# Moving the modulation and gate products beside the gate projections, and reordering the even attention

## The chip, the cores and the metric

One Trainium2 chip, one core. The time is device microseconds of one execution of the whole program, the median of several. Engines: TensorE (PE, matmuls; PEld are its weight loads), VectorE (DVE), ScalarE (ACT), GpSimd (POOL), and SyncE (SP), whose queue issues most of the loads.

## What is computed

Two layers of a diffusion backbone, on 128 prompt tokens and 512 latent tokens, width 1024. The change is in the first (even) layer and in products that the layers' modulation needs. Cut to that:

```python
def layer(x, cvec, l, ctx):
    shift, scale, gate = split(silu(cvec) @ ada_w + ada_b, 3)      # per layer: 1024 -> 3 x 1024
    h = rmsnorm(x, norm_g) * (1.0 + scale) + shift
    out = even_mix(h, ...) or odd_mix(h, ...)
    return x + gate * out

def even_mix(h, ...):
    cq, ckv, kr, g_a, q_b, k_b, v_b, g_b = split_cols(h @ w_in)
    # 8 heads of latent attention (keys of 64 + 32 columns), 8 grouped-query heads (64 columns, 2 key heads)
    o_a = attend(q_a, k_a, v_a) * silu(g_a)        # latent tokens read 128 cached + 512 own keys,
    o_b = attend(q_b, k_b, v_b) * silu(g_b)        # prompt tokens read the 128 prompt keys only
    return concat(o_a, o_b) @ w_out
```

## The kernel before

The program runs stage after stage: modulation of the even layer and its input projections (to 148 us), the gate projections (`even_gates`, L589), the even attention (`attention`, L697), the output projection with the odd layer's norm (`out_proj`, `mid`, from 374 us), then the odd layer. Matrix products in fp32 are made of three products of rounded high and low parts (`mm3`, `lin_feat`): each weight tile of 128 x 1024 is loaded into `raw` (three buffers, taken in turn by all that loads into it), rounded into `whi` on ScalarE (L76), and the rest goes into `wlo` on VectorE, or on GpSimd where `lo_on` says so (L77); then its `raw` buffer is free.

`even_gates` makes eight chunks of 48 matmuls (`lin_feat`, L120), a tanh and a multiply into `og`. Nothing else runs on TensorE there but a few query transposes.

The modulation products of the odd layer are in `ada_cols` (L179): two loads of 512 KB into two `raw` buffers, eight fp32 matmuls on 32-column tiles (L186; 16 records), a copy (L189), and, as the function `rest`, two transposes (L193) and a reduction (L195). The gate vector's product is `ada_gate_part` (L221; one 512 KB load, eight matmuls of 128 columns, L230, a copy), eight times, and `ada_gate_row` sums it and sends it to memory. All of these are issued in the attention: `side(h)` (L863) is called after the value run of head h and issues one `ada_cols` for h below 7 (one more ahead of the first head), and from head 8 on the gate products, the splits `op_split` of the first half of the output's operand (a cast on ScalarE, L890, a subtraction on GpSimd, L891), and from head 12 on one load of output weights each with its low part on GpSimd.

The attention goes over 16 heads (8 latent, 8 grouped). For a head, a score tile (`head_scores`: six matmuls of 320 columns, L619, in latent heads, four in grouped ones) covers 128 of the 512 queries and all 640 keys. It lies in one of two PSUM slots (`s2`). VectorE takes the maximum (L626), ScalarE the exponential with its sum (L629), which frees the slot; VectorE takes the reciprocal (L632), GpSimd multiplies (L639). The result is one of eight `p` buffers. When all four tiles of a head are ready, `head_T` transposes them, key block after key block (5 groups of four transposes, L646, two PSUM slots `t1`), ScalarE or VectorE copies each group to SBUF (L651, L649), and `head_PV` runs the values over them (20 records on 64-column tiles, L657, PSUM `o`, one slot). VectorE multiplies by the gate into `og` (L751). Keys and queries of a head are prepared two heads ahead: a cast and a GpSimd subtraction (L791, L792), transposes (L813, L801).

The prompt's attention runs in four groups of four heads (`prompt_quad`, L661), each in four stages that `attention` places: preparation, scores (L670, in the one slot `o` that the value run needs too) with exponentials (L676), transposes (L683), values (L691).

Inside the attention TensorE's order is the source order: `pe_order` (L158) chains every TensorE instruction of the block to the one before it. On the other engines and on SP's queue a planner orders instructions by when it expects them ready; `issue_after(x)` puts what is traced inside it behind x on x's engine. The order in one head before:

```python
            pt = [self.head_T(T, ps, p, 0, h)]
            ...
                scores(h + 1, 1)
            pt.append(self.head_T(T, ps, p, 1, h))
            scores(h + 1, 2)
            ...
            pt.append(self.head_T(T, ps, p, 2, h))
            done = stage(1)
            scores(h + 1, 3)
            pt += [self.head_T(T, ps, p, k, h) for k in (3, 4)]
            scores(h + 2, 0)
            ...
            for k in range(5):
                self.head_PV(o, V[h], cols[h], pt[k], k)
```

## Time and profile before

| | |
|---|---|
| median of 3 runs | 872.58 us (872.51 to 872.6) |
| the profiled execution | 872.72 us, of which its span is 870.9 |
| instructions | 14357 |
| granted TensorE clock | 0.996 of full speed, mean |
| busiest engine | TensorE, 830.3 us, 95% of the span |

The span runs from the first instruction's start to the last one's end. The times of TensorE's records overlap, since matmuls are pipelined and their ends are modelled; the time from one start to the next says what a step costs. Times in rows are microseconds, unless marked ns.

### The profile page before, as it was taken

Reading aid. Unit: us, or ns where it says so; the run is one execution under the profiler, and the core shown is the slowest. Engines: PE = TensorE matmul, PEld = TensorE weight load, DVE = VectorE, ACT = ScalarE, POOL = GpSimd, SP = SyncE. Lnnn points to the kernel's source line nnn. Section 1 sums busy time; section 2 is a strip of 40 time slices with the busy share of each in tenths; the row PEclk is TensorE's granted clock in tenths of the full one; section 3 lists DMA queues with packets and bytes.
Section 4 is the critical chain, followed back from the end, with each engine's and each line's share of the span. In section 5 each row is a group of like instructions: output and inputs, shape, how many; then the busy total and the mean of one; then the engine's idle time right before and its main releaser. Section 6 shows DMA issues by size and latency. Waiting matters only on the chain.

```text
span 870.9 us, 14357 instructions
## 1 busy us (share of the span) xinstructions
PE 830.3 (95%) x5418; PEld 711.2 (82%) x5418; DVE 532.4 (61%) x1143; ACT 425.6 (49%) x936; POOL 249.8 (29%) x240
## 2 busy tenths in 40 slices
PE   5999999999999998899999999999999999999996
PEld 2778899998788766678888898899988788888786
DVE  3674777324766777535751675377674857676845
ACT  5354356423666866623452235456554656533423
POOL 0010241102755766703320000411310833221121
PEclk9999999999999999999999999999999999999999
DMA  9922222221233112554122213122124222153303
GB/s 343 361 74 73 58 81 79 78 85 52 71 105 117 50 49 74 159 210 142 79 85 102 81 54 109 49 82 84 52 75 135 84 68 69 55 175 113 129 2 121
DMA packets 29641, 88.52 MB, mean 102 GB/s; under 512 B 3752, under 2 KB 6880, under 8 KB 29572
## 3 DMA queue, kind: packets, MB, share of 16 engines
q1 hardware_dynamic: 25904, 83.64, 28.3%
q10 hardware_dynamic: 3668, 3.96, 1.4%
q8 instruction: 43, 0.70, 0.3%
q14 instruction: 26, 0.21, 0.1%
HBM read 80.90 MB, written 6.68 MB: 101 GB/s over the span
## 4 chain that ended last, share of the span: by engine, by line
PE 79%; DVE 7%; POOL 5%; ACT 3%; issue 3%; DMA 2%; SPq 0%; POOLq 0%; ACTq 0%; DVEq 0%
PE acc L83 13%; PE acc L85 13%; PE acc L84 13%; PE acc L120 6%; PE s L619 6%; PE acc L1109 6%; PE o L657 3%; PE t L646 3%; PE pv L1516 2%; PE o L1195 2%; PE ada L186 2%; POOL p L639 1%; PE acc L583 1%; DMA raw<-in_o_wO_dram 1%; PE accA L85 1%
## 5 line engine op out<-in xcount | busy, mean ns | idle before, releaser
L84 PE MATMUL acc<-wlo,Hh 128*128 128x512 f32 (+2 forms) x400 | 149.4, 374 | 0.0
L85 PE MATMUL acc<-whi,Hl 128*128 128x512 f32 (+2 forms) x400 | 148.7, 373 | 0.2 <-DVE Hl L1007 0.2
L83 PE MATMUL acc<-whi,Hh 128*128 128x512 f32 (+2 forms) x400 | 145.6, 380 | 2.4 <-ACT Hh L1005 1.4
L77 DVE TENSOR_TENSOR wlo<-raw,whi 128x1024 fp32r<-128x1024 f32 (+4 forms) x67 | 80.1, 1196 | 94.5 <-ACT whi L76 93.9
L76 ACT CAST whi<-raw 128x1024 fp32r<-128x1024 f32 (+4 forms) x71 | 71.7, 1010 | 128.1 <-PE acc L85 76.1
L626 DVE TENSOR_REDUCE nm<-s 128x1 f32<-128x640 f32 (+1 forms) x104 | 81.0, 779 | 52.1 <-PE s L619 51.2
L639 POOL TENSOR_TENSOR p<-p,rs 128x640 f32<-128x640 f32 x64 | 79.2, 1253 | 95.6 <-issue 52.9
L629 ACT ACTIVATE p<-s,nm 128x640 f32<-128x640 f32 (+1 forms) x104 | 79.4, 765 | 38.4 <-DVE nm L626 36.2
L83 PEld LDWEIGHTS acc<-whi,Hh 128*128 128x128 f32 x400 | 75.5, 190 | 14.6 <-ACT Hh L1005 1.7
L85 PEld LDWEIGHTS acc<-whi,Hl 128*128 128x128 f32 x400 | 76.0, 190 | 13.5 <-DVE Hl L1007 0.4
L84 PEld LDWEIGHTS acc<-wlo,Hh 128*128 128x128 f32 x400 | 76.2, 190 | 12.0 <-DVE wlo L77 0.2
L48 POOL TENSOR_TENSOR rs_r<-rs_h,mhalf 128x1 f32<-128x1 f32 (+4 forms) x39 | 36.9, 950 | 148.8 <-DVE rs_h L47 148.5
L646 PE MATMUL t<-cst,p 128*128 128x128 f32 x320 | 46.9, 276 | 3.1 <-POOL p L639 2.2
L85 PE MATMUL acc<-whi,ol 128*128 128x512 f32 (+1 forms) x124 | 48.0, 387 | 0.0
L84 PE MATMUL acc<-wlo,oh 128*128 128x512 f32 (+1 forms) x124 | 47.8, 387 | 0.0
L83 PE MATMUL acc<-whi,oh 128*128 128x512 f32 (+1 forms) x124 | 47.3, 389 | 0.4 <-DVE z L1418 0.4
L646 PEld LDWEIGHTS t<-cst,p 128*128 128x128 f32 x320 | 36.9, 141 | 8.5 <-POOL p L639 3.6
L651 ACT COPY pT<-t 128x512 f32<-128x512 f32 x56 | 32.0, 587 | 19.1 <-PE t L646 18.5
L632 DVE RECIPROCAL rs<-sm 128x1 f32<-128x1 f32 x104 | 16.6, 159 | 27.3 <-ACT p L629 25.7
L619 PE MATMUL s<-Ka,qh 96*128 96x320 f32 (+1 forms) x128 | 31.6, 329 | 1.7 <-DVE og L127 0.9
L1109 PE MATMUL acc<-Hh,whi 128*128 128x320 f32 x128 | 32.5, 323 | 0.5 <-ACT v L1086 0.5
L1148 POOL TENSOR_TENSOR kdl<-ckd,kdh 128x128 fp32r<-128x128 f32 x8 | 3.6, 461 | 100.9 <-ACT kdh L1147 100.9
(385 smaller groups left out, 1925.0 us busy)
## 6 DMA issues: line engine op xcount, KB each, us to landing
adaw<-in_eada_ss_dram SPq DMA_DIRECT2D x16, 512.0 KB
raw<-in_oada_ss_dram SPq DMA_DIRECT2D x16, 512.0 KB
raw<-in_e_wG_dram SPq DMA_DIRECT2D x8, 512.0 KB
raw<-in_eada_g_dram SPq DMA_DIRECT2D x8, 512.0 KB
raw<-in_e_wO_dram SPq DMA_DIRECT2D x8, 512.0 KB
raw<-in_oada_g_dram SPq DMA_DIRECT2D x8, 512.0 KB
raw<-in_o_wO_dram SPq DMA_DIRECT2D x8, 512.0 KB
xT<-in_xT_dram SPq DMA_DIRECT2D x8, 320.0 KB
```

What stands on the lines that cost most here:

```text
L76: (cp or nc.scalar.copy)(hi[:, 0:m], raw[:, 0:m])
L77: (lo_on or nc.vector).tensor_tensor(out=lo[:, 0:m], in0=raw[:, 0:m], in1=hi[:, 0:m], op=ALU.subtract)
L83: mm(out, lhsT=lh, rhs=rh, start=first, stop=False)
L84: mm(out, lhsT=lh, rhs=rl, start=False, stop=False)
L85: self.mark = mm(out, lhsT=ll, rhs=rh, start=False, stop=last)
L120: mm(acc[j][:, 0:320], lhsT=a[:, k], rhs=b[:, k, j * 320:j * 320 + 320], start=f, stop=l)
L619: self.mark = self.nc.tensor.matmul(out[:, j, 0:w], lhsT=q[0:rows, qcols], rhs=k[0:rows, a:a + w], start=i == 0, stop=i == len(passes) - 1)
L626: nc.vector.tensor_reduce(out=nm, in_=s, axis=AX.XY, op=ALU.max, negate=True)
L629: nc.scalar.activation(out=p[:, 0:n].rearrange("p (a b) -> p a b", a=s.shape[1]), in_=s, func=AF.Exp, bias=nm, accum_out=sm)
L639: self.pm = self.nc.gpsimd.tensor_tensor(out=p, in0=p, in1=rs.to_broadcast([128, 640]), op=ALU.mult)
L646: self.nc.tensor.transpose(tp[:, i * 128:i * 128 + 128], p[i][:, k * 128:k * 128 + 128], self.ident)
L1109: nc.tensor.matmul(acc[j][:, 0:320], lhsT=a[:, k], rhs=b[:, k, j * 320:j * 320 + 320], start=f, stop=l)
```

## The change

`even_gates` gets a further pool and now issues, in each of its eight chunks, the two modulation loads of the odd layer, the gate vector's load into a buffer of its own (`gw`), the gate product and the modulation product; the transposes of a modulation product follow one chunk later. `ada_close` and `ada_gate_row` end it. The attention loses all of these. Its loop has a new order: score tiles are issued further ahead (head h starts with all four of its own and two of the next head's tiles issued), with two score tiles between the transpose groups, one ahead of the first and one right before the value run; keys and queries are prepared three heads ahead; the prompt's stages have fixed heads, and prompt scores come after the first transpose group. The operand's splits and the loads of output weights are put behind the last exponential and the last probability that were issued, and the loads come in the last two heads, two in each, with their low parts on VectorE.

```diff
--- before.py
+++ after.py
@@ -218,10 +218,11 @@
         tt(out=G, in0=G, in1=col(V_OBC), op=ALU.add)
         self.nc.vector.scalar_tensor_tensor(out=G, in0=G, scalar=1.0, in1=col(V_OG), op0=ALU.add, op1=ALU.mult)
 
-    def ada_gate_part(self, L, kk, pool, tag, bufs):
+    def ada_gate_part(self, L, kk, pool, tag, bufs, raw=None):
 
         nc = self.nc
-        raw = self.wp.tile([128, 1024], F32, tag="raw", name="raw", bufs=3)
+        if raw is None:
+            raw = self.wp.tile([128, 1024], F32, tag="raw", name="raw", bufs=3)
         rv = raw.rearrange("p (a b) -> p a b", a=8)
         nc.sync.dma_start(rv, self.A[L + "ada_g"][kk])
         ps = pool.tile([128, 512], F32, tag=tag, name="gps", bufs=bufs)
@@ -318,8 +319,10 @@
         for h in range(2):
             for f in head[0]:
                 f(h, P)
-        self.even_gates(H, L2, ps)
+        L3 = pool("L3", "right")
+        self.even_gates(H, L2, L3, ps)
         ps.release()
+        L3.release()
         L2.release()
         H.release()
         T = pool("T", "left")
@@ -586,13 +589,24 @@
         self.Hh, self.Hl = Hh, Hl
         return qa, kn, Va, krT, Vb, Kb
 
-    def even_gates(self, H, L, ps):
+    def even_gates(self, H, L, W, ps):
+
         Hh, Hl, A = self.Hh, self.Hl, self.A
         self.og = self.st.tile([128, 8, 640], F32, tag="ogx", name="og", bufs=1)
+        rest = None
         for m in range(8):
             acc = self.lin_feat(A["e_wG"][m], Hh, Hl, ps)
+            raws = self.ada_load("o", m)
+            graw = W.tile([128, 1024], F32, name="adag", tag="gw", bufs=1)
+            if rest:
+                rest()
             for j in range(2):
                 self.silu2(self.og[:, m, j * 320:j * 320 + 320], acc[j], [128, 320], L)
+            self.ada_gate_part("e", m, ps, "ada1", 1, graw)
+            rest = self.ada_cols("o", m, ps, "tp", 1, raws, True)
+        rest()
+        self.ada_close()
+        self.ada_gate_row("e", ps, "ada1", 1)
 
     def modulate(self, x, a, b, G, S, kk, hh, hl, pool):
 
@@ -626,8 +640,8 @@
         nc.vector.tensor_reduce(out=nm, in_=s, axis=AX.XY, op=ALU.max, negate=True)
         p = T.tile([128, 640], F32, tag="p", name="p", bufs=bufs)
         sm = T.tile([128, 1], F32, tag="sm", name="sm", bufs=6)
-        nc.scalar.activation(out=p[:, 0:n].rearrange("p (a b) -> p a b", a=s.shape[1]), in_=s, func=AF.Exp,
-                             bias=nm, accum_out=sm)
+        self.ex = nc.scalar.activation(out=p[:, 0:n].rearrange("p (a b) -> p a b", a=s.shape[1]), in_=s, func=AF.Exp,
+                                       bias=nm, accum_out=sm)
         rs = T.tile([128, 1], F32, tag="rs", name="rs", bufs=6)
         nc.vector.reciprocal(rs, sm)
         return p, rs
@@ -699,49 +713,42 @@
         nc = self.nc
         nh = len(cols)
         tiles = {}
-        stages = [(q, i) for q in quads for i in range(4)]
 
         def scores(h, i):
             if h < nh:
                 tiles[h, i] = self.head_scores(T, ps, P[h], i)
 
-        def stage(*kinds):
-            if stages and stages[0][1] in kinds:
-                next(stages.pop(0)[0])
-                return True
-
-        scores(0, 0)
-        scores(0, 1)
-        rest = side(-1)
-        scores(0, 2)
-        rest()
-        scores(0, 3)
-        stage(0)
+        def prepare(h):
+            if h < nh:
+                with self.tc.issue_after(self.pm.ins):
+                    prep[0](h, P)
+                prep[1](h, P)
+
+
+        at = [{a + d: q for a, q in zip((0, 3, 7, 11), quads)} for d in (0, 1, 1, 2)]
+
+        def stage(k, h):
+            if h in at[k]:
+                next(at[k][h])
+
+        for i in range(4):
+            scores(0, i)
+        prepare(2)
         scores(1, 0)
         scores(1, 1)
-        rest = None
         for h in range(nh):
             p = [tiles.pop((h, i)) for i in range(4)]
+            scores(h + 1, 2)
             pt = [self.head_T(T, ps, p, 0, h)]
-            if h + 2 < nh:
-                with self.tc.issue_after(self.pm.ins):
-                    prep[0](h + 2, P)
-            if h:
-                scores(h + 1, 1)
-            if rest:
-                rest()
+            stage(1, h)
             pt.append(self.head_T(T, ps, p, 1, h))
-            scores(h + 1, 2)
-            if h + 2 < nh:
-                prep[1](h + 2, P)
-            pt.append(self.head_T(T, ps, p, 2, h))
-            done = stage(1)
             scores(h + 1, 3)
-            pt += [self.head_T(T, ps, p, k, h) for k in (3, 4)]
+            pt += [self.head_T(T, ps, p, k, h) for k in (2, 3)]
             scores(h + 2, 0)
-            done = done or stage(0, 3)
-            if h == nh - 1:
-                self.ada_gate_row("e", ps, "pr", 1)
+            pt.append(self.head_T(T, ps, p, 4, h))
+            prepare(h + 3)
+            scores(h + 2, 1)
+            stage(3, h)
             o = ps.tile([128, 512], F32, tag="o", name="o", bufs=1)
             for k in range(5):
                 self.head_PV(o, V[h], cols[h], pt[k], k)
@@ -749,8 +756,9 @@
             for j in range(2):
                 g = self.og[r, h // 2, 128 + 256 * j:384 + 256 * j]
                 nc.vector.tensor_tensor(out=g, in0=o[64 * j:64 * j + 64, 0:256], in1=g, op=ALU.mult)
-            rest = side(h)
-            done = done or stage(2)
+            side(h)
+            stage(0, h)
+            stage(2, h)
 
     def stack_q(self, T, ps, srcs, bufs=2):
 
@@ -861,21 +869,17 @@
         quads += [self.prompt_quad(T, ps, prep_gqa(m), Vb, [64 * m] * 4, 4 + 2 * m) for m in range(2)]
 
         def side(h):
-            if h < 7:
-                rest = self.ada_cols("o", h + 1, ps, "pr", 1, split=True)
-                return rest if h < 6 else lambda: (rest(), self.ada_close())
-            if h == 7:
-                return
             if h == 8:
                 EM.release()
                 self.R = self.tc.alloc_tile_pool(name="R1", bufs=1, side="right", reuse_waits="tile")
                 self.sp = {}
-            for i in ((0,), (1,), (2,), (3,), (4, 5), (6,), (7,), ())[h - 8]:
-                self.ada_gate_part("e", i, ps, "pr", 1)
-            if h >= 12:
-                self.op_load("e_wO", 0, h - 12, lo_on=self.nc.gpsimd)
             if 9 <= h < 14:
-                self.op_split(self.R, 0, h - 9)
+                with self.tc.issue_after(self.ex.ins), self.tc.issue_after(self.pm.ins):
+                    self.op_split(self.R, 0, h - 9)
+            if h >= 14:
+                with self.tc.issue_after(self.ex.ins), self.tc.issue_after(self.pm.ins):
+                    for i in (0, 1):
+                        self.op_load("e_wO", 0, 2 * (h - 14) + i)
 
         with self.pe_order():
             self.attention(T, ps, P, prep, [Va] * 8 + [Vb] * 8, [64 * h for h in range(8)] + [64 * (h // 4) for h in range(8)],
```

## Rows read from the trace of the kernel before

**Rows 1.** The page's head and its first part: busy time of each engine, its share of the span and its instructions.

```profile
span 870.9 us, 14357 instructions
PE 830.3 (95%) x5418; PEld 711.2 (82%) x5418; DVE 532.4 (61%) x1143; ACT 425.6 (49%) x936; POOL 249.8 (29%) x240
```

**Rows 2.** Busy time of each engine in three stretches (from:to in us; length, then busy us and instructions by engine, granted clock, share of the DMA engines, GB/s): the gate projections, and the two halves of the even attention.

```profile
147.00:206.00 59.00, 58.45 (x399) 58.15 (x397) 16.86 (x29) 21.80 (x38) 6.75 (x8) 1.00 0.19 63
206.00:300.00 94.00, 90.73 (x781) 75.08 (x782) 65.36 (x141) 62.13 (x148) 59.68 (x48) 1.00 0.26 91
300.00:374.00 74.00, 65.03 (x602) 49.77 (x600) 48.77 (x101) 48.74 (x116) 49.59 (x38) 1.00 0.28 88
```

**Rows 3.** The waits of TensorE from 205 to 374 us: who waited for whom, us in total, times, longest.

```profile
PE s L619 <- ACT p L629: 4.4, 7, 1.7
PE o L657 <- ACT pp L676: 3.1, 3, 1.3
PE t L646 <- POOL p L639: 2.2, 3, 1.5
...
PE t L646 <- ACT pT L651: 0.7, 3, 0.3
```

**Rows 4.** TensorE's timeline (start, duration, what, records, and in brackets the idle time before and what ended it): the first gate matmuls, the first score tiles and the modulation product among them, the first matmul of the output projection.

```profile
148.44 0.54 PE L120 MATMUL acc<-Hh,whi 128*128 128x320 f32 x2
...
206.35 0.56 PE L619 MATMUL s<-Ka,qh 96*128 96x320 f32 x2 [0.90 <-DVE og L127]
...
208.31 1.07 PE L186 MATMUL ada<-raw,sc 128*32 128x256 f32 x16
209.34 0.56 PE L619 MATMUL s<-Ka,qh 96*128 96x320 f32 x2
...
373.98 0.50 PE L83 MATMUL acc<-whi,oh 128*128 128x512 f32 x1
```

**Rows 5.** TensorE's timeline in a latent head: value run, modulation product, transposes of probabilities (L646) and of the product (L193), score tiles (L619, the first rows of each), query transposes (L813).

```profile
223.81 2.38 PE L657 MATMUL o<-pT,Va 128*64 128x256 f32 x20 [1.32 <-ACT pp L676]
226.12 1.07 PE L186 MATMUL ada<-raw,sc 128*32 128x256 f32 x16
227.12 0.66 PE L646 MATMUL t<-cst,p 128*128 128x128 f32 x4
227.53 0.53 PE L619 MATMUL s<-Ka,qh 96*128 96x320 f32 x2
...
228.49 0.38 PE L193 MATMUL ada<-cst,adap 128*128 128x128 f32 x2
228.71 0.60 PE L646 MATMUL t<-cst,p 128*128 128x128 f32 x4
229.06 0.54 PE L619 MATMUL s<-Ka,qh 96*128 96x320 f32 x2
...
230.03 0.60 PE L813 MATMUL qtp<-cst,qa 128*128 128x128 f32 x4
230.47 0.60 PE L646 MATMUL t<-cst,p 128*128 128x128 f32 x4
```

**Rows 6.** The same in grouped heads: value run, gate product (L230), transposes, score tiles.

```profile
304.89 2.38 PE L657 MATMUL o<-pT,Vb 128*64 128x256 f32 x20 [0.53 <-ACT pp L676]
307.20 0.64 PE L230 MATMUL gps<-raw,sc 128*32 128x128 f32 x16
307.77 0.55 PE L646 MATMUL t<-cst,p 128*128 128x128 f32 x3
309.80 0.33 PE L646 MATMUL t<-cst,p 128*128 128x128 f32 x1 [1.48 <-POOL p L639]
309.88 0.84 PE L619 MATMUL s<-Kb,q 128*128 128x320 f32 x4
...
311.58 0.60 PE L646 MATMUL t<-cst,p 128*128 128x128 f32 x4
312.64 0.86 PE L619 MATMUL s<-Kb,q 128*128 128x320 f32 x4 [0.46 <-ACT p L629]
313.33 1.03 PE L646 MATMUL t<-cst,p 128*128 128x128 f32 x8
314.12 0.83 PE L619 MATMUL s<-Kb,q 128*128 128x320 f32 x4
```

**Rows 7.** The chain of waits that ended last, in order of time, at two places of the second half (start, duration, what).

```profile
300.12 4.67 POOL ol L891 x4
...
347.37 3.45 DMA raw<-in_e_wO_dram
350.85 1.05 ACT whi L76
...
351.97 2.37 POOL wlo L77
```

**Rows 8.** What the DMA engines moved: the first 55 us in the columns of rows 2, and the page's GB/s in 40 equal slices.

```profile
0.00:55.00 55.00, 43.78 (x345) 30.07 (x346) 32.13 (x96) 26.54 (x51) 0.20 (x4) 1.00 0.77 290
...
GB/s 343 361 74 73 58 81 79 78 85 52 71 105 117 50 49 74 159 210 142 79 85 102 81 54 109 49 82 84 52 75 135 84 68 69 55 175 113 129 2 121
```

**Rows 9.** From the page's groups of instructions: the low parts of weight tiles on VectorE (count, busy us, mean ns, idle time before and its cause).

```profile
L77 DVE TENSOR_TENSOR wlo<-raw,whi 128x1024 fp32r<-128x1024 f32 (+4 forms) x67 | 80.1, 1196 | 94.5 <-ACT whi L76 93.9
```

**Rows 10.** SP's queue: the load of the gate vector's bias (L238, in `ada_gate_row`, called in the last head).

```profile
37.48 0.33 SPq L238 DMA_DIRECT2D gbias<-in_eada_bg_dram  x1
```

## The prediction

> **What bounds the kernel now.** I read the page first, then the busy time by stage, the waits of TensorE, its timeline with start-to-start times, and the chain of waits. TensorE is busy 95% of the span, VectorE 61% [rows 1]. So a gain can only come from stretches where TensorE is not running, and the stages differ: in the gate projections (147 to 206 us) TensorE is idle for 0.55 us of 59; in the first half of the even attention (206 to 300) for 3.3 of 94; in the second half (300 to 374) for 9.0 of 74 [rows 2]. The list of waits names the causes [rows 3]: score tiles wait for exponentials that hold one of the two score slots (4.4 us, 7 times), value runs wait for the prompt exponentials (3.1, 3 times), transposes wait for GpSimd's normalised probabilities (2.2, 3 times). The attention runs from the first score matmul at 206.35 to the first output-projection matmul at 373.98, 167.6 us; the gates from 148.44 to 206.35, 57.9 us, or 7.2 for each of eight chunks [rows 4].
>
> A wait costs more than the idle time shown, since matmul ends are modelled. Four transposes take 0.35 us undisturbed [rows 5]; those at 311.58 took 1.06 to the next score while the row shows 0.46 idle [rows 6]: 0.25 more. The two windows after 206 hold 12.2 us of idle time [rows 2], 11.9 of it after 206.35; with 7 + 3 + 3 + 3 = 16 waits [rows 3] at 0.25 that makes about **16 us of bubbles** in the attention. Where the second half loses them: five subtractions stand back to back on GpSimd and the probabilities queue behind them; a weight load is waited for 3.45 us on ScalarE, its cast takes 1.05 and its low part 2.37 on GpSimd, and exponentials and probabilities stand behind both [rows 7].
>
> **Part 1, the move.** Eight modulation products (16 matmul records each, 1.00 us [rows 5], 1.03 when entered from full-size scores [rows 4]), their transposes (0.22 [rows 5]), eight gate products (0.57 [rows 6]) and the gate sum (an estimate of 0.6, from the gate product) leave the attention: 8 x (1.02 + 0.22 + 0.57) + 0.6 = 15.1 us. The same 15.1 us arrive in the gate stage, where TensorE has no idle time to hide them. Net zero. It adds copies to ScalarE and a small reduction to VectorE there; the gate window shows them at 21.8 and 16.9 us of 59 [rows 2], so they hide; without that cover only the transpose behind a copy would be late.
>
> Changing from full-size matmuls to 32-column ones: the twelve score records ahead of the product at 208.31 took 1.96 us, two tiles of 0.96 and 0.04 more [rows 4, 5], so entering costs 0.04. I book 0.1 for each of up to eight entries, 0.7 with the start of the stage; bounds 0 and 0.25 (the hidden end of a matmul) for each of 16, so 0 to 4. The Trainium skill, TensorEngine Tiling (Array Packing), section Tiling Modes, says that a change of tiling mode drains TensorE; by that rule, priced at the hidden end of 0.25, the moved products would cost 2 to 4 us more than they gave back, and the time would be 868 to 870. The 0.04 speaks for the low end. Without the rule: 16 entries at the upper bound of 0.25 are 4 us, 3.3 above what is booked, 869.
>
> The loads: per chunk the gate stage now takes four 512 KB tiles (weights, two modulation, one gate) in about 9 us instead of one. That is 2 MB in 9 us, some 230 GB/s; the first 55 us moved 290 on average [rows 8]. Booked at nothing; what covers them is the chunk before (7.2 us), and the price without cover is the second rival.
>
> **Part 2, the order of the attention.** New per-head order: third score of the next head, two transpose groups, its fourth score, two groups, first score of the head after, last group, query transposes three heads ahead, second score, value run. No matmul is added. What happens to the 16 us:
> - *Score slots.* A score tile can start 2.76 us after the one two before it (309.88 to 312.64 [rows 6]). In the grouped heads a score takes 0.69, two transpose groups 0.79 [rows 6]. New distances: third to first 0.69 + 0.79 + 0.69 + 0.79 = 2.96, enough; fourth to second 0.69 + 0.79 + 0.69 + 0.35 = 2.52, short by 0.24 where no query transposes (0.44) lie between. In the latent heads (0.96 a score [rows 5]) it is 3.5, enough. The 4.4 + 1.75 = 6.2 us fall to about 2.
> - *Prompt scores* now come after the first transpose group; a whole head of matmuls (some 4 us) lies between them and the value run that shares their bank, against one or two groups before. 3.1 + 0.75 = 3.9 fall to about 1.
> - *Probabilities.* Splits go one per head behind the last issued probability; the four low parts of the output weights move to VectorE (1.2 us each [rows 9]) at the end, behind the last exponential. 2.2 + 0.75 = 3 fall to 0.5. With no other loads left in the attention the output weights can be fetched early, so the 3.45 us wait goes.
> - *What stays*: transposes waiting for copies, the last head, where no scores are left to fill, and the start: about 3 us.
> - *What is new*: seven score tiles before the first transpose instead of six, at a slot turnaround of 2.76 for two, cost 0.8; 1.2 to 1.5 us for VectorE's and GpSimd's denser queues.
>
> That leaves 2 + 1 + 0.5 + 3 + 0.8 + 1.4 = 8.7 of 16, a gain of 7.3. Bounds: 4 us of bubbles left (gain 12) and all 16 (gain 0); I stay nearer the middle since each price is from a row but queue order is not shown.
>
> **Sum.** -7.3 + 0.7 = -6.6. The profiled execution took 872.72 us (span 870.9 and 1.8 around it), 0.14 above the median of 872.58. 872.6 - 6.6 = **866.0 us**.
>
> **Rivals.** *VectorE or GpSimd paces the grouped heads.* Between 300 and 374 VectorE is busy 48.8 us and GpSimd 49.6 [rows 2]. The four low parts add 4.9 to VectorE: 53.7 us of work in a stretch that should shrink to about 64 (5 us of gate products and some 5 of bubbles less), 84%. For it: the queue is in order, one late reduction delays exponential, slot and score. Against it: durations overlap and GpSimd loses 9.5 us. Another 0.4 us a head, 8 heads: 3 more, 869.
>
> *Slower: the gate stage waits for its weights.* The next chunk's weights share SP's queue with the modulation loads, which must wait until TensorE has used the two buffers. If the weights of the chunk after next stand behind them, each chunk pays: first load 3.45 us, three more at 1.45 to 1.8 (512 KB at 361 GB/s, the best slice of the page, or 290), cast 1.05, low part 1.2 [rows 7 to 9]: 10.1 to 11.1, against 7.2 + 1.8 = 9.0 of cover. That is 1.1 to 2.1 us in each of seven chunks, about 11 in all: 877. It decides from 8.3 us, 1.2 a chunk. Against it: the weights' own buffer is free a chunk earlier, and SP's queue isn't in source order: a bias load written in the last head of the attention was issued at 37.48 us [rows 10]. The Trainium skill, DMA: Bandwidth & Descriptors, section on the anatomy of one DMA, says that a semaphore wait happens on the issuing sequencer ahead of dispatch; so a load behind a waiting one would wait too, which is this rival's mechanism.
>
> *The change doesn't do what it says.* The bubbles come back elsewhere: a transpose waits for its copy where it waited for probabilities, and the prompt exponentials still end late because ScalarE's queue is fuller. Only 1 of 16 us is gained: 872.3, no change. For it: ScalarE and VectorE do the same work in 15 us less. Against it: the three longest waits have causes that are taken away, not shifted [rows 3, 7].
>
> **How the numbers follow.** Forecast 0.58 (861 to 869); every entry drains, 0.03 (869, still faster); an engine paces, 0.13 (about 869, still faster); bubbles come back, 0.09; weights late, 0.13; better than 861, 0.04. A difference of less than 0.2%, 1.7 us, can't be told from no change. Faster 0.58 + 0.03 + 0.13 + 0.04 = 0.78; same 0.09; slower 0.13. The range goes from 860.5 (all of the 12 us gained) to 874.5, past the case of no change; outside lie the late weights and a rest, 0.16. The forecast's own range is 861 to 869.
>
> **What would show it.** Right: the gate stage about 15 to 16 us longer with TensorE still busy throughout; the attention near 145 us (167.6 - 15.1 - 7.3); no TensorE wait on the prompt exponentials above 0.5 us, none on GpSimd's subtractions, no load on the chain in the attention; score waits about 0.3 us, in the grouped heads alone. Wrong: a wait of the gate matmuls for the cast of their weights, in every chunk (second rival); VectorE above 90% from head 8 on (first); waits of transposes on copies that sum to over 5 us (third). Most likely to break the number: a start of the attention that costs several us, or a gate stage that grows by more than 16.

## The result

The changed kernel is slower: 883.15 us (median of 4, 880.95 to 885.77) against 872.59 (872.51 to 873.98), a ratio of 1.0118 (95% interval 1.0086 to 1.0151). The forecast was 866.0, with a range to 874.5. The profiled execution took 880.95 us, 8.2 above that of before; it had the highest mean clock of the four, 0.997 of full speed, the others 0.993, which goes with the higher median (last section).

The page of the changed kernel: its head, the busy time of the engines, and GB/s in 40 equal slices, to be held against [rows 1, 8].

```profile
span 879.1 us, 14378 instructions
PE 834.8 (95%) x5418; PEld 711.0 (81%) x5418; DVE 537.1 (61%) x1147; ACT 427.2 (49%) x936; POOL 241.0 (27%) x236
...
GB/s 342 357 73 72 58 81 101 175 206 221 121 1 2 1 1 1 2 259 122 125 25 133 84 72 89 72 73 73 48 96 133 62 89 68 54 164 114 137 1 120
```

TensorE's share is the same, and the loads have left the attention (slices 12 to 17). The busy time by stage, in the columns of [rows 2], and

```profile
150.40:227.00 76.60, 74.46 (x670) 65.33 (x668) 17.94 (x34) 26.07 (x53) 6.65 (x8) 1.00 0.55 199
227.00:304.00 77.00, 72.34 (x562) 62.01 (x562) 56.95 (x118) 51.47 (x121) 53.00 (x43) 1.00 0.05 16
304.00:384.00 80.00, 70.45 (x546) 54.93 (x543) 60.36 (x119) 55.53 (x126) 47.34 (x39) 1.00 0.08 25
```

show TensorE idle for 2.1 us in the gate stage, where it was 0.55, and for 4.7 + 9.5 in the attention, where it was 12.2: no less than before, with all the products gone. Then the stage bounds, in TensorE's timeline (start, duration, what, in brackets the idle time before and what ended it):

```profile
141.43 0.62 PE L186 MATMUL ada<-raw,sc 128*32 128x256 f32 x2
...
150.41 0.54 PE L120 MATMUL acc<-Hh,whi 128*128 128x320 f32 x2
...
226.95 0.54 PE L633 MATMUL s<-Ka,qh 96*128 96x320 f32 x2
...
383.64 0.50 PE L83 MATMUL acc<-whi,oh 128*128 128x512 f32 x1
```

Against [rows 4] the gates take 76.5 us, not 57.9, and the key projection ahead of them 0.75 more, since a part of the first product (141.43) and two more query transposes were put into it: **19.4 us more** where the forecast had 15.8. The attention takes 156.7 us, not 167.6: **10.9 less** where the forecast had 22.4. What lies ahead of the key projection is 1.2 longer and what lies behind the attention 1.5 shorter, by a stretch of low clock that fell in another place (last section). 19.4 - 10.9 + 1.2 - 1.5 = 8.2.

TensorE's waits in the attention of the changed kernel (who waited for whom, us in total, times, longest), against [rows 3]:

```profile
PE s L633 <- ACT p L643: 3.7, 6, 1.0
PE qtp L854 <- DVE q L814: 2.8, 2, 1.8
PE t L660 <- DVE pT L663: 2.8, 5, 1.0
PE sp L684 <- DVE qp L859: 1.8, 2, 0.9
PE o L671 <- ACT pT L665: 1.6, 1, 1.6
PE t L660 <- ACT pT L665: 1.2, 3, 0.7
```

Value runs no longer wait for prompt exponentials, nor transposes for GpSimd. But four of the six rows are new, and the list sums to 13.9 us.

### The profile page after: what moved, and what is told of

Read it like the earlier page. It is cut to its first block, busy times and chain, and to the rows that moved or that the text cites. A ratio compares the mean times of both kernels' runs of the same rounds, so it can differ in the third digit from the quotient of the medians.

```text
span 879.1 us, 14378 instructions
## 1 busy us (share of the span) xinstructions
PE 834.8 (95%) x5418; PEld 711.0 (81%) x5418; DVE 537.1 (61%) x1147; ACT 427.2 (49%) x936; POOL 241.0 (27%) x236
## 4 chain that ended last, share of the span: by engine, by line
PE 77%; DVE 8%; DMA 6%; ACT 4%; issue 3%; POOL 2%; SPq 0%; POOLq 0%; DVEq 0%; ACTq 0%
PE acc L83 13%; PE acc L85 13%; PE acc L84 13%; PE s L633 7%; PE acc L1113 6%; PE acc L120 4%; PE o L671 4%; PE t L660 3%; DMA raw<-in_e_wG_dram 3%; PE pv L1520 2%; PE o L1199 2%; PE ada L186 1%; ACT p L643 1%; DVE nm L640 1%; DVE wlo L77 1%
## 5 line engine op out<-in xcount | busy, mean ns | idle before, releaser
L77 DVE TENSOR_TENSOR wlo<-raw,whi 128x1024 fp32r<-128x1024 f32 (+4 forms) x71 | 85.6, 1209 | 88.2 <-ACT whi L76 87.7
L83 PEld LDWEIGHTS acc<-whi,Hh 128*128 128x128 f32 x400 | 74.8, 189 | 14.6 <-ACT Hh L1009 1.7
L84 PEld LDWEIGHTS acc<-wlo,Hh 128*128 128x128 f32 x400 | 75.5, 189 | 12.2 <-DVE wlo L77 0.3
L660 PE MATMUL t<-cst,p 128*128 128x128 f32 x320 | 45.1, 275 | 4.1 <-DVE pT L663 2.8
L1113 PE MATMUL acc<-Hh,whi 128*128 128x320 f32 x128 | 32.5, 323 | 0.5 <-ACT v L1090 0.5
L120 PE MATMUL acc<-Hh,whi 128*128 128x320 f32 x128 | 30.7, 317 | 2.0 <-ACT whi L76 2.0
L938 ACT ACTIVATE junk<-xt 128x512 bf16<-128x512 f32 (+1 forms) x21 | 12.8, 610 | 40.1 <-DVE xt L936 34.8
```

The lines of the kernel that those rows point to most:

```text
L77: (lo_on or nc.vector).tensor_tensor(out=lo[:, 0:m], in0=raw[:, 0:m], in1=hi[:, 0:m], op=ALU.subtract)
L83: mm(out, lhsT=lh, rhs=rh, start=first, stop=False)
L84: mm(out, lhsT=lh, rhs=rl, start=False, stop=False)
L120: mm(acc[j][:, 0:320], lhsT=a[:, k], rhs=b[:, k, j * 320:j * 320 + 320], start=f, stop=l)
L660: self.nc.tensor.transpose(tp[:, i * 128:i * 128 + 128], p[i][:, k * 128:k * 128 + 128], self.ident)
L1113: nc.tensor.matmul(acc[j][:, 0:320], lhsT=a[:, k], rhs=b[:, k, j * 320:j * 320 + 320], start=f, stop=l)
```

## The experiments

Three things were changed at once: the place of the **products** (in the gate stage, in the attention, or left out), the **loop** (the order of scores, transposes, values, prompt stages), the **side work** (splits and output weights: old as before, new behind the last exponential and probability, weights in the last two heads, low parts on VectorE). The table has them apart; the order inside the gate stage comes after. "Attention" is the profiled time from the first score to the output projection. Times are medians in us; before it ran at 872.4 to 873.8 beside them.

| loop | side work | products left out | in the attention | in the gate stage |
|---|---|---|---|---|
| old | old | 869.3 (attention 164.5) | before, 872.6 (167.6) | 891.4 (164.4) |
| old | new | 859.8 (154.2) | 870.4 (165.0) | 879.9 (155.8) |
| new | new | 861.5 (156.6) | 874.0 (169.5) | changed, 883.2 (156.7) |

The attentions of 164.4, 164.5 and 155.8 us each hold stretches of low clock in and behind waits: at a mean of 0.97 in the first two some 5 us of TensorE's work were not granted, in the third 1.7 (0.77 from 377.5 to 385 us). The other six ran at full clock.

### Which part costs: products, loop or side work

**Old loop and old side work, products in the gate stage.** The changed kernel with the loop of before (its product calls removed) and

```diff
-            if h >= 14:
-                with self.tc.issue_after(self.ex.ins), self.tc.issue_after(self.pm.ins):
-                    for i in (0, 1):
-                        self.op_load("e_wO", 0, 2 * (h - 14) + i)
+            if h >= 12:
+                self.op_load("e_wO", 0, h - 12, lo_on=self.nc.gpsimd)
```

> The products in the gate stage as in the changed kernel, the attention in the order of the kernel before (its output weights from head 12 on too). Theory A, the new order is at fault for part of the loss: the gate stage is some 19.5 us longer than before, the attention 15.1 us shorter, so 872.6 + 4.4 = 877. Rival B, the products filled waits of the old attention, and taking them away is what costs: the attention is only 10 to 11 us shorter, as in the changed kernel, so 881 to 882.

891.43 (887.23 to 891.77), as rival B or worse: the attention is only 3.2 us shorter than before. **The same without products:**

```diff
+        self.nc.gpsimd.memset(self.gs["o"], 0.0)
+        self.nc.gpsimd.memset(self.gp, 0.0)
         for m in range(8):
             acc = self.lin_feat(A["e_wG"][m], Hh, Hl, ps)
-            raws = self.ada_load("o", m)
...
-            self.ada_gate_part("e", m, ps, "ada1", 1, graw)
-            rest = self.ada_cols("o", m, ps, "tp", 1, raws, True)
```

> The modulation products of the odd layer and the gate products of the even one are left out altogether (their results are set to zero); the attention is in the order of before. This prices the products where they stood. Theory A (their price in the old attention is the sum of their own times): 872.6 - 15.1 = 857.5, less 0.6 because the gate sum is kept: 858. Rival B (they filled waits there): only 10 to 11 us are saved, 862.

869.29 (868.82 to 871.83): 14.5 us of TensorE's work taken away (the gate sum stays, at the end of the gate stage) saved 3.3. The reason stands on GpSimd in that run (timeline: start, duration, what), and in TensorE's transposes:

```profile
294.22 7.03 POOL L77 TENSOR_TENSOR wlo<-raw,whi 128x1024 fp32r<-128x1024 f32 x3
301.20 4.96 POOL L885 TENSOR_TENSOR ol<-og,oh 128x512 fp32r<-128x512 f32 x4
306.11 2.47 POOL L647 TENSOR_TENSOR p<-p,rs 128x640 f32<-128x640 f32 x2
```
```profile
313.14 0.47 PE L654 MATMUL t<-cst,p 128*128 128x128 f32 x1 [4.18 <-POOL p L647]
```

With the products' loads gone the first output weights are issued at 180 us, not at 336, the planner runs three low parts and four subtractions back to back, and the probabilities queue 12 us behind them. In these waits the clock falls, to 0.50 from 310 to 315 us. The run above shows the same bunch, from 314 us on. The products' loads had kept that apart; in before the bunch is the subtractions of [rows 7] (five in the trace, 6.2 us from 298.88; the row has the last four).

**New loop, new side work, no products** (the changed kernel with the same removal).

> The same products left out, the attention in the new order. The difference to the kernel with the old order and no products is the new order alone. Theory A: 4 us slower than that one, about 862, with waits of the prompt's query transposes in heads 8 and 12, a burst of casts in the last head and 3 to 4 us of waits for score slots at the start. Rival B: the same or faster than that one. Against the changed kernel it prices the products in the gate stage: 19 to 20 us if the waits and entries seen there are all caused by them.

861.46 (859.39 to 864.77). So 7.8 us faster than the old order: the gain that the forecast promised, but only against an order spoiled by the removal. Against the changed kernel, the products cost 21.7 in the gate stage by the medians; 19.4 of it show in the stage itself, most of the rest is a stretch of low clock at 20 us. **Old loop with the new side work, no products:**

```diff
-            if h >= 12:
-                self.op_load("e_wO", 0, h - 12, lo_on=self.nc.gpsimd)
             if 9 <= h < 14:
-                self.op_split(self.R, 0, h - 9)
+                with self.tc.issue_after(self.ex.ins), self.tc.issue_after(self.pm.ins):
+                    self.op_split(self.R, 0, h - 9)
+            if h >= 14:
+                with self.tc.issue_after(self.ex.ins), self.tc.issue_after(self.pm.ins):
+                    for i in (0, 1):
+                        self.op_load("e_wO", 0, 2 * (h - 14) + i)
```

> The kernel with the old order and without the products (869.3 us), but with the operand's splits and the output weights placed as in the changed kernel: behind the last exponential and the last probability, the weights in the last two heads, low parts on VectorE. In the trace of the old order without the products, three low parts (7.0 us) and four subtractions (5.0 us) stand back to back on GpSimd from 294 to 306 us, and transposes wait for the probabilities behind them until 313. Theory A, this bunch is what the old order loses, and the placing of the side work is what the new one gains: 861 to 862, as the new order without the products (861.5). Theory B, the order of scores, transposes and prompt stages gains most of it: 866 or more.

859.79 (857.9 to 862.66): theory A. The side work's place made all of the 7.8 us; the loop made none, and the attention (154.2) is 2.4 shorter than with the new one. **The kernel before with the new side work** (the same edit, products where they were):

> The kernel before, products in the attention where they were, with one part of the change: the operand's splits and the output weights behind the last exponential and the last probability, the weights in the last two heads with low parts on VectorE. In the trace of before the five subtractions on GpSimd (6.2 us from 298.88) and the four weight loads lie on waits that sum to 6 us. Theory A, these waits go and the products keep filling others: attention 161 to 162, time 866 to 867. Theory B, the products then fill nothing: the old loop without products and with this side work took 154.2 us in the attention, plus 15.1 is 169.3, time 874.

870.43, ratio 0.9965 (0.9952 to 0.9978): a gain, but of 2.7 us, between the theories. The bunch is gone (on GpSimd two probabilities and no subtraction start between 299 and 305), and the attention is 165.0: the products cost 165.0 - 154.2 = 10.8 there, so 4.3 of their 15.1 us don't show. The whole attention without the products and with them, in the columns of [rows 2]:

```profile
205.80:360.10 154.30, 140.64 (x1101) 116.36 (x1101) 117.88 (x233) 105.90 (x246) 100.39 (x81) 1.00 0.04 12
205.85:370.86 165.01, 154.37 (x1381) 124.75 (x1381) 117.34 (x243) 110.80 (x262) 100.32 (x81) 1.00 0.25 84
```

TensorE's idle time falls from 13.7 to 10.6: 3.0 us of waits are filled. The other 1.3 or so are the difference between the 15.1 of the forecast's sum and the 13.7 by which the busy time grows. **Old loop, new side work, products in the gate stage:**

> The changed kernel with the old loop of the attention: products in the gate stage, splits and weights placed as in the change. Without products the old loop's attention took 154.2 us in the profile where the new one took 156.6. Theory A, the new loop costs 2.4 us here too: 883.2 - 2.4 = 880.8. Theory B, it costs nothing: 883.

879.94 (877.59 to 882.67, 6 runs), 3.2 below the changed kernel: theory A (a loss of 2.4) fits better, though the intervals of the two ratios to before touch (1.0055 to 1.0090, and 1.0086 to 1.0151). **New loop and side work, products back in the attention,** one behind the first transpose group of each head; first with one load of output weights a head, then with the weights in the last two heads:

```diff
             pt = [self.head_T(T, ps, p, 0, h)]
+            rest = fill(h)
             stage(1, h)
...
             pt += [self.head_T(T, ps, p, k, h) for k in (2, 3)]
+            if rest:
+                rest()
             scores(h + 2, 0)
```

> The gate stage of before; the products back in the attention, each after the first transpose group of a head, in the new order, with the prompt groups after heads 0, 3, 6 and 10 and one load of output weights a head from head 10 to 13. If the products fill waits of the new order as they did of the old one, the attention takes 155.3 (the run with shifted prompt groups) + some 7 of the 15.1 us - 2.4 (casts out of the last head) = 160, and the time is 865. If they don't, it takes 168 and the time is 873.

> The changed kernel with the move undone: the gate stage of before, the products in the attention after the first transpose group of a head, new order, prompt groups after heads 0, 3, 6 and 10, output weights in the last two heads as in the change. In the run with one load of weights a head the gate products waited 7.1 us for loads that stood in the ring behind weights whose casts were held back; here the weights come after. Theory A, the products fill waits of the new order: 155.3 + 8 to 10 = 164 us of attention, time 869. Theory B, they fill nothing: 170.4, time 875.

880.45 and 873.97 (872.45 to 876.2, 10 runs). In the second the attention is 169.5, 12.9 above the new loop without products (14.2 above the run with shifted prompt groups, below): near theory B. This kernel differs from before and its new side work in the loop, in where the products stand and in the prompt's heads, so the 12.9 is no price of the loop alone. What the second expectation says of the first run, that its gate products waited for loads, was wrong. The lines of the first at one of the two waits:

```profile
330.10 0.44 PE L850 MATMUL qtp<-cst,qb 128*128 128x128 f32 x2
...
331.90 1.80 DVE L77 TENSOR_TENSOR wlo<-raw,whi 128x1024 fp32r<-128x1024 f32 x1
...
334.59 0.43 DVE L855 TENSOR_TENSOR qp<-qtp,qp 64x256 fp32r<-64x256 f32 x1 [0.24 <-ACT qp L854]
...
335.12 0.64 PE L231 MATMUL gps<-raw,sc 128*32 128x128 f32 x16 [3.56 <-issue]
```

The gate product starts 0.1 us after VectorE has read the last of the prompt's query transposes, which lie in the one bank `pr` that the product needs; the low part of a weight tile stands ahead of that read. It waited for the bank, not for its load.

**The same bank in the changed kernel.** Its two new waits for `q` are of that kind: keys and queries are prepared three heads ahead, so in heads 7 and 11 the next queries' transposes take the bank (309.02) right ahead of the prompt's (313.55):

```profile
309.02 0.60 PE L809 MATMUL qtp<-cst,qb 128*128 128x128 f32 x4
...
312.71 0.69 DVE L814 TENSOR_TENSOR q<-qtp,q 64x512 fp32r<-64x512 f32 x1 [0.37 <-ACT q L813]
...
313.55 0.41 PE L854 MATMUL qtp<-cst,qb 128*128 128x128 f32 x2 [1.03 <-DVE q L814]
...
316.18 0.89 PE L684 MATMUL sp<-Kb,qp 128*128 128x128 f32 x6 [0.88 <-DVE qp L859]
```

```diff
-        at = [{a + d: q for a, q in zip((0, 3, 7, 11), quads)} for d in (0, 1, 1, 2)]
+        at = [{a + d: q for a, q in zip((0, 3, 6, 10), quads)} for d in (0, 1, 1, 2)]
```

> The changed kernel with the last two groups of prompt heads prepared one head earlier (after heads 6 and 10, not 7 and 11), where no query transposes of the head three ahead hold the one bank that both need. If the bank is the cause, the two waits of the prompt's transposes (2.8 us) go, and with them what the records hide, 3 to 4 us in all, so 879 to 880. If the cause is VectorE's queue in general, the wait moves to the prompt scores behind and less than 1 us is gained.

881.2 (880.03 to 883.51), by the medians 2 us, inside the spread of both. The wait for `q` is gone from the list, the one for `qp` (1.8) stays, and transposes now wait 1.6 for the copies of the prompt's. The attention is 155.3, 1.4 less: the bank was the cause of that wait, and half of its 2.8 us went on to the next.

### Why the gate stage grew by 19.4 and not 15.1

The waits of gate matmuls in the changed kernel and of SP's modulation loads for TensorE, one of the matmuls' waits with the cast ahead of it, and SP's queue around it:

```profile
PE acc L120 <- ACT whi L76: 2.0, 2, 1.0
...
SPq L175 <- PE ada L186: 12.9, 4, 5.5
```
```profile
176.43 1.04 ACT L76 CAST whi<-raw 128x1024 fp32r<-128x1024 f32 x1 [3.30 <-DMA raw<-in_e_wG_dram]
...
177.52 0.56 PE L120 MATMUL acc<-Hh,whi 128*128 128x320 f32 x2 [0.94 <-ACT whi L76]
```
```profile
171.08 0.33 SPq L175 DMA_DIRECT2D raw<-in_oada_ss_dram  x1
171.51 0.37 SPq L75 DMA_DIRECT2D raw<-in_e_wG_dram  x1
172.86 0.33 SPq L227 DMA_DIRECT2D adag<-in_eada_g_dram  x1
...
182.42 0.33 SPq L175 DMA_DIRECT2D raw<-in_oada_ss_dram  x1
182.85 0.37 SPq L75 DMA_DIRECT2D raw<-in_e_wG_dram  x1
```

The weights' load stands right behind a modulation load that waits for TensorE: the mechanism of the second rival. The Trainium skill says it too (DMA: Bandwidth & Descriptors, the anatomy of one DMA: the semaphore wait is on the issuing sequencer), and the trace agrees, 0.43 us from the one issue to the other. It bites in two chunks, not in seven. In other executions the wait was longer: 2.6 us in the run with shifted prompt groups.

**The products on data already in SBUF** (their 24 loads left out):

```diff
-            raws = self.ada_load("o", m)
+            raws = [Hh[:, 4 * i:4 * i + 4, 0:256].bitcast(F32) for i in range(2)]
...
-            self.ada_gate_part("e", m, ps, "ada1", 1, graw)
+            self.ada_gate_part("e", m, ps, "ada1", 1, Hh[:, :, 0:128].bitcast(F32))
```

> The changed kernel, but the moved products read data that already lies in SBUF, and their 24 loads are left out. TensorE does the same work. If late weights and loads make the gate stage's excess, it is 57.9 + 15.1 + 1 = 74 us, time 880 or less, with little spread between runs; if the scattered entries into 32-column products make it, it stays at 76 us and the time at 882 to 883.

878.69 (876.42 to 882.2). The first score starts at 222.48; without products it started at 205.86, with the same clock: 16.6 us for the products, against 19.4 with their loads. So 2.8 us go with the loads, 1.5 are the rest. The run leaves out more than the transfers: with no load to wait for, two of the modulation products ran ahead of the key projection (115.01 and 132.52), which then began 3.2 us later than without products (142.48, not 139.26). They cost no less there, so the 16.6 still counts them in full; but the 2.8 holds what the other place is worth, too.

**The weights in the buffer that the gate load had** and **TensorE's order fixed on top of it:**

```diff
-            graw = W.tile([128, 1024], F32, name="adag", tag="gw", bufs=1)
+            graw = W.tile([128, 1024], F32, name="rawg", tag="gw", bufs=1)
+            acc = self.lin_feat(A["e_wG"][m], Hh, Hl, ps, raw=graw)
...
+        order = self.pe_order()
+        order.__enter__()
```

> The changed kernel with the extra buffer of the gate stage given to the gate weights; the gate product's load takes the shared ring with the modulation loads instead. If the weights come late because their buffer in the ring is taken, the waits of the gate matmuls for the cast (2.0 us in the changed kernel's profile, 3.8 and 3.9 in two others) go: 880. If they come late because their load stands on the queue behind a modulation load that waits for TensorE, the waits stay: 883.

> The same, and TensorE's order in the gate stage fixed as written: after the 48 matmuls of a chunk come the transposes, the gate product and the modulation product together. The loads of weights then stand two chunks ahead on the queue. If late weights and the entries into 32-column products (each costs the full-size matmul ahead some 0.1 us and the one behind 0.1) make the gate stage's excess over 57.9 + 15.1 us, 2 to 4 us of it go: 879 to 881. If the transfers themselves are the limit (2 MB a chunk), the matmuls wait all the same: 883 or more.

885.08 and 885.97, both worse; the waits for the cast fall to 0 and 0.9 us. What came instead are single waits, with the clock down to 0.50 at each, at the stage's start, 4.9 us (a transpose for the copy ahead of it) and 5.9 (query transposes for the bank that the first head's still held). Two versions with a changed start had a wait of 5.5 us on the same bank and one of 8.0 on the first cast. In the second the load was held for a write of VectorE that ends at 147.05 us (it was issued at 147.08), which fits a buffer that lies where a pool has just been released; the cast then stood behind ScalarE's casts of keys and queries, which run from 150.23 to 157.41:

```diff
+            if h:
+                self.prep_ps = lambda: ps.tile([128, 1024], F32, tag="tp", name="qtp", bufs=1)[:, 0:512]
...
+            with self.tc.issue_after(self.wd.ins):
+                raws = self.ada_load("o", m)
```

> The changed kernel with three edits in the gate stage: TensorE's order is fixed from the first product on (after the 48 matmuls of a chunk: transposes, gate product, modulation product), the weights have the buffer of their own, and the products' loads of a chunk stand behind its weights on the queue; the second head's query transposes take another bank, so that the first product doesn't wait for the split of the first. In the run with fixed order alone, the stage behind its start went at 8.9 us a chunk, the 7.05 of the matmuls and 1.8 of the products and nothing else. Theory A, order and queue made the excess: the stretch from the first matmul of the last key projection to the first score is 66.6 + 15.1 = 81.7 us against 86.0, time 879. Theory B, the transfers make it: 883 or more.

> The changed kernel with TensorE's order fixed in the whole gate stage, weights in a buffer of their own and ahead of the products' loads on the queue, and the second head's query transposes in another bank. Theory A, order and queue made the excess: from the first matmul of the last key projection to the first score 66.6 + 15.1 + 0.6 = 82.3 us against 86.0, time 879.5. Theory B, the products cost more in themselves here: 85 us or more, 883.

883.44 and 887.54; 886.52 with the old loop, where 877 had been expected. **With the first chunk's weights in the old ring,** old loop and new side work:

```diff
-            graw = W.tile([128, 1024], F32, name="rawg", tag="gw", bufs=1)
+            graw = W.tile([128, 1024], F32, name="rawg", tag="gw", bufs=1) if m else None
```

> Old loop, new side work, products in the gate stage in a fixed order, the first chunk's weights through the shared ring (loaded early), the others through their own buffer. If nothing holds up the start: 66.6 + 15.1 + 1 = 82.7 us to the first score, attention 155, profile 870.9 + 16.1 - 12.6 = 874.4, median 875 to 876: the move loses in itself against the same kernel with the products in the attention (870.4). If it comes to 871 or less, the move was not at fault, only its order.

876.62, ratio 1.0049 (1.0032 to 1.0067). Two turns of the mended stage:

```profile
176.53 0.38 PE L194 MATMUL ada<-cst,adap 128*128 128x128 f32 x2
176.85 0.65 PE L232 MATMUL gps<-raw,sc 128*32 128x128 f32 x16
177.31 1.05 PE L187 MATMUL ada<-raw,sc 128*32 128x256 f32 x16
...
185.43 0.38 PE L194 MATMUL ada<-cst,adap 128*128 128x128 f32 x2
```

A chunk with its products takes 8.9 us, 7.1 + 1.8, and key projection and gates together 83.0, against 66.6 before: 16.4, that is 15.1 + 1.3, with all 24 loads: in this order the transfers hide. The move loses even so (this run against 870.43 with the products in the attention), since the same products cost less there.

### A version that beats both

Of the parts of the change only the side work gained. Its run had a gate product that waited 1.5 us for the bank in head 11, and casts in the last head. The first edit takes both out, the second the bank's wait alone:

```diff
-            for i in ((0,), (1,), (2,), (3,), (4, 5), (6,), (7,), ())[h - 8]:
+            for i in ((0,), (1, 2), (3,), (), (4, 5), (6,), (7,), ())[h - 8]:
...
-            if h >= 14:
+            if 13 <= h < 15:
...
-                        self.op_load("e_wO", 0, 2 * (h - 14) + i)
+                        self.op_load("e_wO", 0, 2 * (h - 13) + i)
```

> The kernel before with the new placing of splits and weights (870.4 us), and two edits: no gate product in head 11, where the prompt's query transposes hold the bank it needs (it waited 1.5 us there), and the output weights behind heads 13 and 14, out of the last head, where their casts stood ahead of the copies that transposes wait for (1.1 us). If both waits go and nothing takes their place: 868. If the gate products then wait elsewhere, or the casts hold up the exponentials of the last head: 870 or more.

> The kernel before with the new placing of splits and weights (870.4 us), and no gate product in head 11, where the bank it needs is held. The output weights stay in the last two heads. If the wait of 1.5 us there goes: 869. If it gains nothing again (870.4 or more), the bank's wait only covered another one.

870.8: with the weights behind head 13 a score waits for an exponential that stands behind the casts.

```profile
360.27 0.86 PE L619 MATMUL s<-Kb,q 128*128 128x320 f32 x4 [2.33 <-ACT p L629]
```

And **867.77** (867.16 to 871.36, 7 runs), ratio 0.9955 (0.9939 to 0.9971): faster than before by 0.45%, and than the changed kernel by 15 us. Against the new side work alone (0.9965, 0.9952 to 0.9978) the intervals overlap; the wait of 1.5 us is gone from the list, and the attention is 164.1, 0.9 shorter, so the products cost 9.9 there.

## Why the prediction was wrong

**Which step failed.** "The same 15.1 us arrive in the gate stage, where TensorE has no idle time to hide them. Net zero." The gate stage has 0.55 us of idle time, and the attention had 12.2 us of it [rows 2]; the prediction read both and then priced the products at their own time in both places. Measured, they cost 9.9 and 10.8 us in the attention (old loop, new side work), and 19.4 in the gate stage, 16.4 when mended. So 4 to 5 us are missing on the side that the products left, and 4 on the side that they came to. Of the miss of 14.8 us in the profiled time (880.95 against 866.1), 4.3 are the products' price in the attention, 7.1 the order's gain that did not come, and 3.6 the gate stage (19.4 against 15.8).

**The gain of 7.3 us from the order** came to nothing: with the products in place, side work -2.6 (167.6 to 165.0), new loop +2.4 (154.2 to 156.6): 0.2. With the 10.8 of the products, 167.6 - 2.6 - 10.8 + 2.4 = 156.6, which is what the changed kernel shows. Term by term:

- *Probabilities* (3 to 0.5, weights fetched early): right; GpSimd is off the list. It is the only term that gained, and the old loop has it as well.
- *Score slots* (6.2 to 2): right inside the loop, where 0.2 us of the 3.7 are left. 3.5 us are ahead of the first value run, where tiles of the next head follow in two slots and no product lies between; before it was 0.7. So the start cost 2.8 more, booked at 0.8: that term was mis-sized.
- *Prompt scores* (3.9 to 1): the wait for the prompt exponentials went, as said. In its place came the prompt's query transposes and scores, 2.8 + 1.8 us. The prediction said of a removed wait what is late next in the value run only, and did not list who holds the one bank `pr`.
- *The end* (booked with what stays): the casts behind the last exponential come at once, ahead of copies that the last value runs and transposes wait for, 3.5 us of waits from 369 us on, the last 14.6 of the attention, where the last 14.6 of before had 1.8:

```profile
372.65 2.93 ACT L76 CAST whi<-raw 128x1024 fp32r<-128x1024 f32 x3
...
376.12 0.65 PE L671 MATMUL o<-pT,Vb 128*64 128x256 f32 x4 [1.56 <-ACT pT L665]
```

**The gate stage.** Entries into 32-column products were booked at 0.7: all that is not loads or the products' own time is 1.5, or 1.3 in a fixed order, inside the bounds. So the rule that a change of tiling mode drains TensorE (the Trainium skill, TensorEngine Tiling (Array Packing), Tiling Modes) made no price of 4 us here. The loads were booked at nothing; 2.8 us went with them, and a fixed order with all of them took 3.0 less.

**The rivals.** Late weights (877) had the right mechanism at a quarter of its price (2.8 of 11 us); "the bubbles come back" (872.3) had the right outcome for the attention. They came together, and the prediction had given them chances as if only one could. VectorE did not pace: it is busy for 60.4 of the attention's last 80 us.

## What to carry to other kernels

Price a move by the stage it leaves and the stage it enters, not by the moved work's own time: in a stage with waits the work is partly free, in a full one it is not, and its loads come with it. When work is taken out, look at what its loads and buffers had held back; a planner may bunch what is now ready early. Before changing several orders at once, try each alone: here one of three gained 2.7 us, and the other two cost four to five times as much.

## What the runs showed of the hardware

The granted clock falls to the lower level, 1.2 GHz (0.50 of full speed), for some microseconds behind an idle stretch of TensorE, not behind each, and not in the same place in each execution. In the changed kernel it fell behind a wait of 1.84 us at 20 us, and stayed at 1.00 behind one of 1.78 at 349.89. Busy time in windows (from:to, length, busy us and instructions by engine, granted clock, DMA share, GB/s): first the changed kernel, then before.

```profile
17.50:20.00 2.50, 0.64 (x9) 0.19 (x10) 2.03 (x6) 0.98 (x3) 0.00 (x0) 1.00 1.02 407
20.00:22.50 2.50, 2.50 (x19) 1.19 (x19) 0.75 (x1) 0.75 (x2) 0.00 (x0) 0.61 1.04 425
22.50:25.00 2.50, 2.50 (x18) 2.07 (x11) 1.32 (x4) 0.90 (x2) 0.00 (x0) 0.71 1.02 419
```
```profile
444.00:448.00 4.00, 2.49 (x19) 2.05 (x17) 2.15 (x6) 2.80 (x7) 0.05 (x1) 1.00 0.00 0
448.00:452.00 4.00, 3.87 (x18) 3.87 (x19) 1.08 (x2) 1.09 (x2) 2.65 (x6) 0.57 0.00 0
```

The share that was not granted is 0.39 x 2.5 + 0.29 x 2.5 = 1.7 us of work in the one, 0.43 x 4 = 1.7 in the other. Executions of one kernel differ by how many such stretches they had: before took 871.0 us at a mean of 0.999 and 876.6 at 0.992. A long wait thus costs more than its length: in the run whose first gate matmul waited 8.0 us, the 48 matmuls of that chunk took 9.6 us to the gate product behind them, not 7.0.

```profile
155.00:160.00 5.00, 1.47 (x5) 1.24 (x6) 2.52 (x3) 3.39 (x7) 2.04 (x2) 0.50 0.00 0
160.00:165.00 5.00, 5.00 (x24) 5.00 (x25) 0.52 (x1) 1.05 (x1) 0.00 (x0) 0.64 0.32 105
...
158.53 0.90 PE L121 MATMUL acc<-Hh,whi 128*128 128x320 f32 x2 [7.96 <-ACT whi L77]
...
168.16 0.65 PE L232 MATMUL gps<-raw,sc 128*32 128x128 f32 x16
```
